# Value, query and gate projections in 512-column matmuls, and all of PSUM opened stage by stage, in a hybrid encoder layer

## The chip, the cores and the metric

The kernel runs on one core of a Trainium2 chip. The metric is device time in microseconds (us) of one execution; a kernel's time is the median of its runs. Engines are named as in the profile: PE is TensorE (PEld its weight load), DVE VectorE, ACT ScalarE, POOL GpSimd, SP SyncE, which issues most DMAs.

## What is computed

One encoder layer over 512 tokens of width 1024, in float32. The part that matters here is the first half:

```python
u = x * (1.0 + sc1) + sh1
proj = u @ w_in[l]
(rq, rff, rfb, ri, rg, aq, ak, av, gate_rec, gate_att) = jnp.split(proj, split_points, axis=-1)
y_rec = hgrn2_bidirectional(rq, rff, rfb, ri, rg, ...) @ w_rec_branch[l]
q = rotary(aq...); k = rotary(ak...); v = av
y_att = windowed_gqa_with_sink(q, k, v, attn_sink[l]) @ w_attn_branch[l]
merged = jax.nn.sigmoid(gate_rec) * y_rec + jax.nn.sigmoid(gate_att) * y_att
```

Then come an output projection with a layer norm, and a convolutional feed-forward block with another. `ri` are the values of the recurrent mixer (512 features), `rg` its output gate (512), `aq` the queries of the attention (512), `ak` and `av` its keys and values (128 each), `rff`, `rfb` and `rq` forget gates and queries of the recurrence (4 heads of 128).

## The kernel before, in words

Every product with weights is done in three matmuls: activations and weights are each split in a rounded part (`hi`, type fp32r, made by ScalarE) and a rest (`lo`, made by VectorE), and `mm3` (L118) adds hi x hi, hi x lo and lo x hi in PSUM. Weights come by DMA as tiles of 1 MB (`w_tile`, two buffers) and are split in two pieces of 128x1024 (`w_split`, L109; four buffers each for hi and lo).

The program has four parts in time. The **head** (to L330) computes the modulation and `u`, and with it the first projections, for heads 0 and 1 of the recurrence, into six PSUM banks `first0` to `first5` (L305). The **scan** (L781 to L796) does the recurrence for two pairs of heads (`scan_pair`, L622): seven levels of 64-column products (`pl`, one pair of banks each, two pairs in turn), then state products (`kt`, `st`) and outputs (`po`). Its VectorE work per level (multiplying `kb` and `qb` by the totals, and masked copies out of PSUM) needs longer than its matmuls. So the remaining projections run between the levels as a **background stream** (`Stream`, L382): a list of items, each with a load and a generator of steps of three matmuls. `scan_pair` yields a number of nanoseconds (STEP is 4600, STEPD 3400, STEPK 4000, STEPS 2600, STEPA 4200; LEAD 13600 stands ahead of the scan), and `drive` (L424) runs as many steps as fill it by the estimate that each step yields. When an item starts, the load of the next is issued. `bg.until(n)` runs the stream until n items are done. Then comes the **attention** (L808 to L993), which uses up the rest of the stream, and then the rest of the layer.

Two kinds of items exist. `proj_fm` (L353) computes features by tokens: weights stationary, 512 tokens moving, one bank of 512 columns over 8 steps. `proj_tm` (L366) computes tokens by features: a token block of `u` stationary, 256 columns of weights moving. A bank holds two token blocks of 256 features, so an item of 256 features is 32 steps, 96 matmuls, two banks. Seven items are of this kind: values (2), keys and values of the attention (1), queries (2), output gate (2). Their results leave PSUM by `use_v`, `use_kv`, `use_q`, `use_rg` (L738 to L756).

PSUM has eight banks of 512 float32 columns. A pool `ps` (L81) with three banks, tag `mm`, lives through the kernel and serves the stream. The five others are opened anew in each stage (`psum_stage`, L84): `ps_start` (two `sc` and three `at` banks), `ps_scan` (two pairs and one `sc`), `ps_rest` (three `at`, two `sc`). A tile scheduler orders the instructions of ScalarE, VectorE and GpSimd by priorities and sets the waits; matmuls marked `kp` stay in program order.

Of the kernel before, what the change touches and what calls it, by code (L numbers as in the profile page):

```python
# [8 lines left out]
F32 = mybir.dt.float32  # L9
F32R = mybir.dt.float32r  # L10
I32 = mybir.dt.int32
AF = mybir.ActivationFunctionType
# [4 lines left out]
P = 128  # L17
# [44 lines left out]
def encoder_layer(  # L62
# [18 lines left out]
    ps = ctx.enter_context(tc.tile_pool(name="ps", bufs=3, space=PSUM))  # L81
# [8 lines left out]
    def mm_ps(name):  # L90
        return ps.tile([P, 512], F32, tag="mm", name=name, bufs=3)
# [11 lines left out]
    banks["sc"] = 2  # L103
# [33 lines left out]
    with tc.tile_pool(name="st", bufs=1) as st:  # L137
# [168 lines left out]
        for p in range(len(pieces)):  # L306
# [3 lines left out]
            if not more:  # L310
                raw = w_tile()
                kp(nc.sync.dma_start(raw.rearrange("p (k n) -> p k n", n=256), w_in_k[:, :, C_RI:C_RI + 256]))
# [3 lines left out]
            else:  # L316
                lows(p, u32)
                ri_parts = w_split_late(raw)
# [47 lines left out]
    def proj_tm(use):  # L366
# [13 lines left out]
        return steps  # L380

# [42 lines left out]
    def drive(fg):  # L424
        for ns in fg:
            bg.run(ns)
# [93 lines left out]
    with tc.tile_pool(name="mx", bufs=1) as mx:  # L520
# [217 lines left out]
        def use_v(hh):  # L738
            return lambda b, a: nc.scalar.copy(v_rec[:, 2 * b:2 * b + 2, 256 * hh:256 * hh + 256], a)
# [5 lines left out]
        def use_q(i):  # L745
            return lambda b, a: nc.scalar.copy(
                qk_raw[:, 2 * b:2 * b + 2, 4 * i:4 * i + 4].rearrange("p b h d -> p b (h d)"), a)

        def use_rg(hh):
            def use(b, a):  # L750
                th = hp.tile([P, S], F32, tag="th", name="th", bufs=2)
                tv = th.rearrange("p (i n) -> p i n", i=2)
                nc.scalar.activation(tv, a, AF.Tanh, scale=0.5)
                nc.vector.scalar_tensor_tensor(out=rgs[:, 2 * b:2 * b + 2, 256 * hh:256 * hh + 256], in0=tv,
                                               scalar=1.0, in1=a, op0=ALU.add, op1=ALU.mult)
            return use  # L756

        ri_load = lambda: ri_parts
        bg.add(ri_load, proj_tm(use_v(0)))
# [3 lines left out]
        bg.add(load_cols(C_RI + 256), proj_tm(use_v(1)))  # L763
        bg.add(load_cols(C_AK), proj_tm(use_kv))
        bg.add(load_cols(C_AQ), proj_tm(use_q(0)))
        bg.add(load_cols(C_AQ + 256), proj_tm(use_q(1)))
        for hh in range(2):
            bg.add(load_cols(C_RG + 256 * hh), proj_tm(use_rg(hh)), ada_hook)
# [13 lines left out]
        banks["sc"] = 1  # L782
        bg.run(LEAD)
        drive(scan_pair(0, 1, lambda L: None))
        cos2, sin2 = rotary_tables()
        bg.until(5)
# [565 lines left out]
```

## Time and profile before

| | us |
|---|---|
| median of 3 runs | 804.8 (803.76 to 805.15) |
| the profiled execution | 803.86 |
| its span, first to last instruction | 802.1 |
| TensorE busy | 782.2 (98%) |
| VectorE busy | 559.6 (70%) |
| ScalarE busy | 358.4 (45%) |
| GpSimd busy | 71.2 (9%) |

A busy TensorE is not one at its peak: a matmul's row lasts from its start to its modelled end, some 390 ns for 512 columns, while the next one starts earlier. The distance between starts is what a matmul costs when they follow each other. In the rows, times are in us from the span's start unless marked ns; `<-` before a name in brackets says what ended the engine's idle time.

### The profile page before, as it was taken

How to read it: one execution, taken by the hardware profiler on the slowest of the kernel's cores; microseconds unless marked ns; L12 is line 12 of the kernel's file. 1: busy time of each engine (PE TensorE's matmuls, PEld its weight loads, DVE VectorE, ACT ScalarE, POOL GpSimd, SP SyncE). 2: the span in 40 equal slices, each digit the busy share in tenths (PEclk: the TensorE clock that was granted, in tenths of full speed). 3: DMA queues.
4: the chain of work that ended last, by engine and by line, in shares of the span. 5: the costliest groups of instructions: out<-in, count | busy, mean ns of one | idle time of the engine just before them, and what ended most of it. 6: DMA issues, size and time to landing. Idle time of an engine off the chain costs nothing.

```text
span 802.1 us, 11578 instructions
## 1 busy us (share of the span) xinstructions
PE 782.2 (98%) x4606; PEld 660.8 (82%) x4606; DVE 559.6 (70%) x881; ACT 358.4 (45%) x576; POOL 71.2 (9%) x98
## 2 busy tenths in 40 slices
PE   5999999999999999999999999999999999999996
PEld 4779889999878777788889988888888888888885
DVE  5879994699486756648766787777665677546437
ACT  3565754653276575533345544434544444112120
POOL 3340000000000000200000683000000000000000
PEclk9999999999999999999999999999999999999999
DMA  9983331122543503686403343464423333332302
GB/s 270 301 231 93 107 105 54 53 83 78 158 145 118 158 1 105 234 222 231 130 29 106 88 123 105 157 210 106 134 80 102 105 105 132 106 105 79 105 1 105
DMA packets 110757, 99.45 MB, mean 124 GB/s; under 512 B 3452, under 2 KB 98032, under 8 KB 110704
## 3 DMA queue, kind: packets, MB, share of 16 engines
q1 hardware_dynamic: 109024, 94.38, 39.7%
q0 software_dynamic: 1664, 4.33, 1.7%
q8 instruction: 36, 0.59, 0.3%
q14 instruction: 17, 0.14, 0.1%
q10 hardware_dynamic: 16, 0.00, 0.0%
HBM read 96.61 MB, written 2.10 MB: 123 GB/s over the span
## 4 chain that ended last, share of the span: by engine, by line
PE 93%; DVE 3%; DMA 1%; ACT 1%; SPq 1%; issue 0%; DVEq 0%
PE up L121 10%; PE up L120 10%; PE up L119 10%; PE dn L119 5%; PE dn L120 5%; PE dn L121 5%; PE fm L119 5%; PE fm L121 5%; PE fm L120 5%; PE tm L119 4%; PE tm L121 3%; PE tm L120 3%; PE pl L618 2%; PE wo L119 2%; PE wo L121 2%; PE wo L120 2%
## 5 line engine op out<-in xcount | busy, mean ns | idle before, releaser
L114 DVE TENSOR_TENSOR w_lo<-raw,w_hi 128x1024 fp32r<-128x1024 f32 x114 | 140.6, 1247 | 103.8 <-ACT w_hi L113 103.7
L113 ACT CAST w_hi<-raw 128x1024 fp32r<-128x1024 f32 x114 | 118.6, 1050 | 146.9 <-PE dn L121 76.0
L119 PE MATMUL up<-u_hi,w_hi 128*128 128x512 f32 (+1 forms) x384 | 142.8, 372 | 0.0
L120 PE MATMUL up<-u_lo,w_hi 128*128 128x512 f32 (+1 forms) x384 | 142.6, 371 | 0.0
L121 PE MATMUL up<-u_hi,w_lo 128*128 128x512 f32 (+1 forms) x384 | 142.6, 371 | 0.0
L120 PEld LDWEIGHTS up<-u_lo,w_hi 128*128 128x128 f32 x384 | 72.3, 188 | 12.6
L119 PEld LDWEIGHTS up<-u_hi,w_hi 128*128 128x128 f32 x384 | 72.3, 188 | 12.5
L121 PEld LDWEIGHTS up<-u_hi,w_lo 128*128 128x128 f32 x384 | 72.3, 188 | 12.4
L119 PE MATMUL dn<-w_hi,g_hi 128*128 128x512 f32 (+1 forms) x198 | 72.5, 366 | 0.0
L120 PE MATMUL dn<-w_lo,g_hi 128*128 128x512 f32 (+1 forms) x198 | 72.5, 366 | 0.0
L121 PE MATMUL dn<-w_hi,g_lo 128*128 128x512 f32 (+1 forms) x198 | 72.4, 366 | 0.0
L119 PE MATMUL fm<-u_hi,w_hi 128*128 128x512 f32 x176 | 70.4, 400 | 0.0
L121 PE MATMUL fm<-u_hi,w_lo 128*128 128x512 f32 x176 | 68.8, 391 | 0.0
L120 PE MATMUL fm<-u_lo,w_hi 128*128 128x512 f32 x176 | 68.8, 391 | 0.0
L119 PE MATMUL tm<-w_hi,u_hi 128*128 128x256 f32 x224 | 64.8, 289 | 0.0
L121 PE MATMUL tm<-w_hi,u_lo 128*128 128x256 f32 x224 | 63.3, 283 | 0.0
L120 PE MATMUL tm<-w_lo,u_hi 128*128 128x256 f32 x224 | 63.3, 283 | 0.0
L437 DVE SCALAR_TENSOR_TENSOR ada<-raw,silu_c,ada 128x1024 f32<-128x1024 f32 x32 | 41.0, 1282 | 12.5 <-DMA raw<-in_w_ada_dram 12.2
L1215 ACT CAST g_hi<-cv 128x512 fp32r<-128x512 f32 x22 | 13.7, 621 | 69.1 <-DVE cv L1214 69.1
L119 PEld LDWEIGHTS tm<-w_hi,u_hi 128*128 128x128 f32 x224 | 42.8, 191 | 0.8
L120 PEld LDWEIGHTS tm<-w_lo,u_hi 128*128 128x128 f32 x224 | 43.0, 192 | 0.1
L121 PEld LDWEIGHTS tm<-w_hi,u_lo 128*128 128x128 f32 x224 | 42.9, 191 | 0.0
(284 smaller groups left out, 1448.9 us busy)
## 6 DMA issues: line engine op xcount, KB each, us to landing
raw<-in_w_up_dram SPq DMA_DIRECT2D x44, 512.0 KB, 5.3
raw<-in_w_ada_dram SPq DMA_DIRECT2D x16, 1024.0 KB, 5.3
raw<-in_w_in_dram SPq DMA_DIRECT2D x15, 1024.0 KB, 5.3
raw<-in_w_down_dram SPq DMA_DIRECT2D x10, 1024.0 KB, 5.0
aw<-in_w_ada_dram SPq DMA_DIRECT2D x32, 256.0 KB, 5.3
raw<-in_w_out_dram SPq DMA_DIRECT2D x4, 1024.0 KB, 4.8
wq<-in_w_in_dram SPq DMA_DIRECT2D x24, 128.0 KB, 4.8
raw<-in_w_in_dram SPq DMA_DIRECT2D x6, 512.0 KB, 4.7
```

The lines of the kernel that those rows point to most:

```text
L113: nc.scalar.copy(hi[:, 0:n], raw[:, o:o + n])
L114: nc.vector.tensor_tensor(out=lo[:, 0:n], in0=raw[:, o:o + n], in1=hi[:, 0:n].bitcast(F32), op=ALU.subtract)
L119: pin(nc.tensor.matmul(o, lhsT=sh, rhs=mh, start=start, stop=False))
L120: pin(nc.tensor.matmul(o, lhsT=sh, rhs=ml, start=False, stop=False))
L121: pin(nc.tensor.matmul(o, lhsT=sl, rhs=mh, start=False, stop=stop))
L437: nc.vector.scalar_tensor_tensor(out=acc, in0=raw[:, j * D:(j + 1) * D], scalar=silu_c[:, 2 * k2 + j:2 * k2 + j + 1], in1=acc, op0=ALU.mul ...
L618: kp(nc.tensor.matmul(dst[64 * a:64 * a + 64, q_:q_ + 64], lhsT=keys[:, k_:k_ + 64], rhs=queries[:, q_:q_ + 64], start=True, stop=True, ti ...
L1215: nc.scalar.copy(g_hi[i], cv[0])
```

## The change

Values, queries and output gate become three pairs of half items. An item of a pair loads four of the eight 128-row blocks of the weights, 512 columns wide (`load_wide`), and adds their products for all four token blocks into four banks (`proj_wide`); the second item of the pair adds the other four row blocks, and each bank leaves PSUM as soon as it is complete. Each step is three matmuls of 512 columns and yields 680. The pool `ps` is gone: the `mm` banks belong to the stage, three in `ps_start`, four in `ps_scan` (whose `sc` bank goes), three in `ps_rest`. The item that the head prepares is now keys and values of the attention, with the two value items behind it; then follow, as before, the features of heads 2 and 3, then queries and gate. The counts in `until` and `need` follow the new list.

```diff
--- before.py
+++ after.py
@@ -78,7 +78,6 @@
     cn = ctx.enter_context(tc.tile_pool(name="cn", bufs=1))
     wp = ctx.enter_context(tc.tile_pool(name="wp", bufs=4))
     big = ctx.enter_context(tc.tile_pool(name="big", bufs=1))
-    ps = ctx.enter_context(tc.tile_pool(name="ps", bufs=3, space=PSUM))
     banks = {}
 
     def psum_stage(name):
@@ -88,7 +87,7 @@
         banks["pool"] = banks["ctx"].enter_context(tc.tile_pool(name=name, bufs=1, space=PSUM))
 
     def mm_ps(name):
-        return ps.tile([P, 512], F32, tag="mm", name=name, bufs=3)
+        return banks["pool"].tile([P, 512], F32, tag="mm", name=name, bufs=banks["mm"])
 
     def sc_ps(name):
         return banks["pool"].tile([P, 512], F32, tag="sc", name=name, bufs=banks["sc"])
@@ -100,7 +99,7 @@
         return banks["pool"].tile([P, 2, 512], F32, tag="pair", name=name, bufs=2)
 
     psum_stage("ps_start")
-    banks["sc"] = 2
+    banks["sc"], banks["mm"] = 2, 3
 
 
     def w_tile():
@@ -309,13 +308,13 @@
             more = p + 1 < len(pieces)
             if not more:
                 raw = w_tile()
-                kp(nc.sync.dma_start(raw.rearrange("p (k n) -> p k n", n=256), w_in_k[:, :, C_RI:C_RI + 256]))
+                kp(nc.sync.dma_start(raw.rearrange("p (k n) -> p k n", n=256), w_in_k[:, :, C_AK:C_AK + 256]))
             if more:
                 nxt = prepare_w(p + 1)
                 acc = gather(p + 1, lambda: lows(p, u32))
             else:
                 lows(p, u32)
-                ri_parts = w_split_late(raw)
+                kv_parts = w_split_late(raw)
             mms = first_mm(p, parts)
             for _ in range(SPLIT[p]):
                 next(mms)
@@ -378,6 +377,34 @@
                             use(b, acc.rearrange("p (i n) -> p i n", i=2))
                         yield 327
         return steps
+
+    def load_wide(col, kh):
+        def load():
+            raw = w_tile()
+            nc.sync.dma_start(raw.rearrange("p (k n) -> p k n", n=512), w_in_k[:, 4 * kh:4 * kh + 4, col:col + 512])
+            return [w_split(raw, 1024 * h, first=False) for h in range(2)]
+        return load
+
+    def proj_wide(use):
+
+        accs = []
+
+        def half(kh):
+            def steps(parts):
+                for tb in range(NTB):
+                    t = slice(tb * P, (tb + 1) * P)
+                    if kh == 0:
+                        accs.append(mm_ps(f"tw{tb}"))
+                    for j in range(4):
+                        k = 4 * kh + j
+                        hi, lo = parts[j // 2]
+                        n = slice((j % 2) * 512, (j % 2) * 512 + 512)
+                        mm3(accs[tb], u_hi[:, k, t], u_lo[:, k, t], hi[:, n], lo[:, n], k == 0, k == KT - 1, kp)
+                        if k == KT - 1:
+                            use(tb, accs[tb])
+                        yield 680
+            return steps
+        return half(0), half(1)
 
     class Stream:
         def __init__(self):
@@ -735,37 +762,33 @@
                                          accum_out=rstat[:, tb, h:h + 1])
                 nc.scalar.copy(o_tok[:, :, h], po[:, e].rearrange("p (b d) -> p b d", d=P))
 
-        def use_v(hh):
-            return lambda b, a: nc.scalar.copy(v_rec[:, 2 * b:2 * b + 2, 256 * hh:256 * hh + 256], a)
+        def use_v(tb, a):
+            nc.scalar.copy(v_rec[:, tb], a)
 
         def use_kv(b, a):
             nc.scalar.copy(qk_raw[:, 2 * b:2 * b + 2, 8:10].rearrange("p b h d -> p b (h d)"), a[:, :, 0:128])
             nc.scalar.copy(v_att[:, 2 * b:2 * b + 2], a[:, :, 128:256])
 
-        def use_q(i):
-            return lambda b, a: nc.scalar.copy(
-                qk_raw[:, 2 * b:2 * b + 2, 4 * i:4 * i + 4].rearrange("p b h d -> p b (h d)"), a)
-
-        def use_rg(hh):
-            def use(b, a):
-                th = hp.tile([P, S], F32, tag="th", name="th", bufs=2)
-                tv = th.rearrange("p (i n) -> p i n", i=2)
-                nc.scalar.activation(tv, a, AF.Tanh, scale=0.5)
-                nc.vector.scalar_tensor_tensor(out=rgs[:, 2 * b:2 * b + 2, 256 * hh:256 * hh + 256], in0=tv,
-                                               scalar=1.0, in1=a, op0=ALU.add, op1=ALU.mult)
-            return use
-
-        ri_load = lambda: ri_parts
-        bg.add(ri_load, proj_tm(use_v(0)))
+        def use_q(tb, a):
+            nc.scalar.copy(qk_raw[:, tb, 0:8].rearrange("p h d -> p (h d)"), a)
+
+        def use_rg(tb, a):
+            th = hp.tile([P, S], F32, tag="th", name="th", bufs=2)
+            nc.scalar.activation(th, a, AF.Tanh, scale=0.5)
+            nc.vector.scalar_tensor_tensor(out=rgs[:, tb], in0=th, scalar=1.0, in1=a, op0=ALU.add, op1=ALU.mult)
+
+        first_load = lambda: kv_parts
+        wide_v, wide_q, wide_g = proj_wide(use_v), proj_wide(use_q), proj_wide(use_rg)
+        bg.add(first_load, proj_tm(use_kv))
+        for kh in range(2):
+            bg.add(load_wide(C_RI, kh), wide_v[kh])
         for h in (2, 3):
             bg.add(load_cols(C_RFF + h * P, C_RFB + h * P), proj_fm(lambda f, a, h=h: gate_f(f, h, a)))
             bg.add(load_half(C_RQ + h * P), proj_fm(lambda f, a, h=h: silu_q(h, a), nf=1))
-        bg.add(load_cols(C_RI + 256), proj_tm(use_v(1)))
-        bg.add(load_cols(C_AK), proj_tm(use_kv))
-        bg.add(load_cols(C_AQ), proj_tm(use_q(0)))
-        bg.add(load_cols(C_AQ + 256), proj_tm(use_q(1)))
-        for hh in range(2):
-            bg.add(load_cols(C_RG + 256 * hh), proj_tm(use_rg(hh)), ada_hook)
+        for kh in range(2):
+            bg.add(load_wide(C_AQ, kh), wide_q[kh])
+        for kh in range(2):
+            bg.add(load_wide(C_RG, kh), wide_g[kh], ada_hook)
         gr_a = yin.tile([P, 2, S], F32, name="gr_a")
         gr = [gr_a[:, i] for i in range(2)]
 
@@ -779,25 +802,25 @@
             gate_f(1, j, first[2 + j])
             silu_q(j, first[4 + j])
         psum_stage("ps_scan")
-        banks["sc"] = 1
+        banks["mm"] = 4
         bg.run(LEAD)
-        drive(scan_pair(0, 1, lambda L: None))
+        drive(scan_pair(0, 3, lambda L: None))
         cos2, sin2 = rotary_tables()
-        bg.until(5)
+        bg.until(7)
 
         def turn_qk(L):
             if L == 64:
                 bg.until(9)
                 rope(range(2))
 
-        drive(scan_pair(1, 6, turn_qk))
+        drive(scan_pair(1, 3, turn_qk))
         rope(range(2, 4))
         bg.until(11)
         dump("qk_raw", qk_raw)
 
         hp_ctx.close()
         psum_stage("ps_rest")
-        banks["sc"] = 2
+        banks["sc"], banks["mm"] = 2, 3
 
         grp_pool = ph1.enter_context(tc.tile_pool(name="grp", bufs=1, side="right"))
         gr_b = grp_pool.tile([P, KT - 2, S], F32, name="gr_b")
```

**The opening of the scan's stage, TensorE.** `first0` to `first5` are the head's accumulators, `tm0` is the first bank of the stream's first item. Before:

```order
L294 MATMUL first4_233<-u_lo_71,w_hi_555 128x512
L294 MATMUL first5_234<-u_lo_71,w_hi_555 128x512
L119 MATMUL tm0_741<-w_hi_610,u_hi_70 128x256 [waits Activation_49]
L120 MATMUL tm0_741<-w_lo_611,u_hi_70 128x256 [waits DVE_49]
L121 MATMUL tm0_741<-w_hi_610,u_lo_71 128x256
```

and now:

```order
L293 MATMUL first4_230<-u_lo_68,w_hi_552 128x512
L293 MATMUL first5_231<-u_lo_68,w_hi_552 128x512
L118 MATMUL tm0_737<-w_hi_607,u_hi_67 128x256 [waits DVE_49,PE_49]
L119 MATMUL tm0_737<-w_lo_608,u_hi_67 128x256
L120 MATMUL tm0_737<-w_hi_607,u_lo_68 128x256
```

`tm0` has moved from the pool that lives through the kernel to the first place in the new stage's pool; its first matmul waits for VectorE's count 124 and for TensorE's `first5`, where it waited for ScalarE's tanh of `first0`. VectorE's order there is the same as before but for line numbers; row 124 of the list, the reader of `first5`, is the sixth of these:

```order
L616 SCALAR_TENSOR_TENSOR lvl_mask_675<-xf_681,xg_682 128x128 [waits DVE_49]
L626 TENSOR_SCALAR f0_701<-th_713,f_mul_643,f_add_644 128x512 [waits Activation_49]
L626 TENSOR_SCALAR f0_701<-th_716,f_mul_643,f_add_644 128x512 [waits Activation_49]
L571 TENSOR_SCALAR ang_1524<-inv_1491,pos_f_1489 128x32 [waits Pool_49]
L659 TENSOR_SCALAR kb0_866<-f0_701 128x2048 [waits DVE_49]
L636 SCALAR_TENSOR_TENSOR q0_708<-th_719,first5_231 128x512 [waits Activation_49]
L660 TENSOR_TENSOR ks0_868<-kb0_866 128x1024 [waits DVE_49]
L637 TENSOR_SCALAR q0_708<-q0_708 128x512 [waits DVE_49]
```

These are gates and queries of heads 0 and 1 (`th` is a tanh of ScalarE) and the first operations of `scan_pair`.

**ScalarE behind it.** `qk_raw` and `v_att` take `tm0` out of PSUM; `kc` and `qc` are copies of level 1 and 2 of the scan. Before (where the first item was values, `v_rec`):

```order
L598 ACTIVATE th_719<-first3_232 128x512 [waits DVE_49]
L739 COPY v_rec_658<-tm0_741 128x2x256 [waits PE_49]
L608 ACTIVATE th_722<-first5_234 128x512 [waits DVE_49]
L670 COPY kc0_1_914<-kb0_863 128x1024 [waits DVE_49]
L113 CAST w_hi_843<-raw_841 128x1024 [waits DMAHW4_49,PE_49]
L739 COPY v_rec_658<-tm1_791 128x2x256 [waits PE_49]
L113 CAST w_hi_939<-raw_936 128x1024 [waits DMAHW6_49,DMAHW5_49]
```

and now:

```order
L625 ACTIVATE th_716<-first3_229 128x512 [waits DVE_49]
L635 ACTIVATE th_719<-first5_231 128x512 [waits DVE_49]
L697 COPY kc0_1_910<-kb0_866 128x1024 [waits DVE_49]
L697 COPY qc0_1_911<-qb0_867 128x1024 [waits DVE_49]
L697 COPY qc0_2_971<-qb0_867 128x1024 [waits DVE_49]
L769 COPY qk_raw_660<-tm0_737 128x2x128 [waits PE_49,Activation_49]
L770 COPY v_att_661<-tm0_737 128x256
```

The copies out of `tm0` stood ahead of the tanh of `first5` and of `kc`, and now stand behind both `qc`.

**The opening of the attention's stage, TensorE.** `fm` are features of a gate, `pk0` the transposes of the first keys. Before:

```order
L119 MATMUL fm0_2503<-u_hi_70,w_hi_2317 128x512
L120 MATMUL fm0_2503<-u_lo_71,w_hi_2317 128x512
L121 MATMUL fm0_2503<-u_hi_70,w_lo_2318 128x512
L833 MATMUL pk0_2525<-ident_72,kk0_2519 128x128 [waits PE_49,Activation_49]
L833 MATMUL pk0_2525<-ident_72,kk0_2519 128x128
```

and now:

```order
L118 MATMUL fm1_2107<-u_hi_67,w_hi_1895 128x512
L119 MATMUL fm1_2107<-u_lo_68,w_hi_1895 128x512
L120 MATMUL fm1_2107<-u_hi_67,w_lo_1896 128x512
L856 MATMUL pk0_2201<-ident_69,kk0_2194 128x128 [waits Activation_49]
L856 MATMUL pk0_2201<-ident_69,kk0_2194 128x128
```

The `fm` that runs ahead of `pk0` is now one that began in the scan's stage (`fm1`), and `pk0` waits for its reader on ScalarE.

## Rows read from the trace of the kernel before

**Rows 1.** The page: the chain that ended last, shares of the span by engine.

```profile
PE 93%; DVE 3%; DMA 1%; ACT 1%; SPq 1%; issue 0%; DVEq 0%
```

**Rows 2.** TensorE's timeline where the head ends: start us, us, engine, line, op, out<-in, shapes, count.

```profile
57.15 1.52 PE L294 MATMUL first<-u_lo,w_hi 128*128 128x512 f32 x6
58.51 0.28 PE L119 MATMUL tm<-w_hi,u_hi 128*128 128x256 f32 x1
```

**Rows 3.** TensorE in the scan: timeline of `tm` and `fm`; the page's group of narrow matmuls.

```profile
69.90 0.28 PE L121 MATMUL tm<-w_hi,u_lo 128*128 128x256 f32 x1
...
99.97 0.40 PE L120 MATMUL fm<-u_lo,w_hi 128*128 128x512 f32 x1
...
104.06 0.39 PE L120 MATMUL fm<-u_lo,w_hi 128*128 128x512 f32 x1
...
L119 PE MATMUL tm<-w_hi,u_hi 128*128 128x256 f32 x224 | 64.8, 289 | 0.0
```

**Rows 4.** TensorE's timeline in the output projection: two `wo` matmuls, four apart.

```profile
400.76 0.39 PE L120 MATMUL wo<-w_lo,m_hi 128*128 128x512 f32 x1
...
401.67 0.39 PE L121 MATMUL wo<-wo_hi,m_lo 128*128 128x512 f32 x1
```

**Rows 5.** VectorE's timeline after the head.

```profile
58.42 1.21 DVE L114 TENSOR_TENSOR w_lo<-raw,w_hi 128x1024 fp32r<-128x1024 f32 x1
...
66.42 1.22 DVE L632 TENSOR_SCALAR kb<-f 128x2048 f32<-128x2048 f32 x1
67.56 0.68 DVE L609 SCALAR_TENSOR_TENSOR q<-th,first 128x512 f32<-128x512 f32 x1
68.16 1.22 DVE L633 TENSOR_TENSOR ks<-kb 128x1024 f32<-128x1024 f32 x1
```

**Rows 6.** ScalarE's timeline: a `v_rec` copy, the last tanh of `first`, `qc` of level 2.

```profile
65.31 0.58 ACT L739 COPY v_rec<-tm 128x512 f32<-128x512 f32 x1
65.94 0.60 ACT L608 ACTIVATE th<-first 128x512 f32<-128x512 f32 x1
...
77.69 1.16 ACT L670 COPY qc<-qb 128x1024 f32<-128x1024 f32 x1 [1.33 <-DVE qb L660]
```

**Rows 7.** TensorE at the head, then windows at the end: us, busy by engine, PEclk, DMA.

```profile
11.00 0.80 PE L296 MATMUL first<-u_hi,w_hi 128*128 128x512 f32 x1 [1.17 <-ACT u_hi L262]
...
16.13 0.79 PE L296 MATMUL first<-u_hi,w_hi 128*128 128x512 f32 x1
...
18.00 0.63 PE L296 MATMUL first<-u_hi,w_hi 128*128 128x512 f32 x1
18.43 0.63 PE L297 MATMUL first<-u_hi,w_lo 128*128 128x512 f32 x1
18.85 2.15 PE L294 MATMUL first<-u_lo,w_hi 128*128 128x512 f32 x6
20.85 0.39 PE L296 MATMUL first<-u_hi,w_hi 128*128 128x512 f32 x1
...
794.00:798.00 4.00, 0.86 (x8) 0.65 (x6) 3.54 (x11) 0.20 (x1) 0.00 (x0) 1.00 0.34 128
798.00:802.00 4.00, 0.00 (x0) 0.00 (x0) 1.30 (x4) 0.00 (x0) 0.00 (x0) 0.55 0.37 131
```

**Rows 8.** TensorE's timeline at the attention's first transposes: [idle before <-releaser] at the end.

```profile
223.97 0.39 PE L121 MATMUL fm<-u_hi,w_lo 128*128 128x512 f32 x1
224.55 0.44 PE L833 MATMUL pk<-ident,kk 128*128 128x128 f32 x2 [0.19 <-ACT kk L819]
225.84 0.33 PE L833 MATMUL pk<-ident,kk 128*128 128x128 f32 x1 [0.85 <-DVE kk L820]
```

**Rows 9.** TensorE's timeline in the scan: two levels' products.

```profile
84.36 1.15 PE L618 MATMUL pl<-qc,kc 128*64 128x64 f32 x32
...
91.11 1.09 PE L618 MATMUL pl<-qc,kc 128*64 128x64 f32 x30
```

**Rows 10.** VectorE's timeline in the scan: the masked copy of a level.

```profile
86.60 1.50 DVE L678 COPY_PREDICATED sc<-lvl_mask,pl 64x512 f32<-64x512 int32 x2
```

## The prediction

> **What bounds the kernel now.** First the page's busy shares and its chain of waits: the chain that ended last runs over TensorE for 93% of the span [rows 1]. So a gain or a loss counts where TensorE issues matmuls or stands still, and other engines count where TensorE waits for them. Next the list of TensorE's matmuls with their starts, over the stretch that the change rewrites. The head ends with six matmuls of `first`, and the first `tm` follows at 58.51 us without a gap [rows 2]. From there to `pk` at 224.55 us the starts follow each other at the pace of the matmuls; the first waits to see are those at `pk` [rows 8]. So in this stretch the end moves one for one with TensorE's issue time. Then the paces. A 512-column `fm` starts every (104.06 - 99.97)/18 = 0.227 us; a 256-column `tm` every (69.90 - 58.51)/95 = 0.120 us, which is 0.240 us for 512 columns [rows 2, 3]. A narrow matmul therefore costs some 6 ns that the wide form pays once where the narrow one pays twice. That is all that width alone can give. Last, VectorE and ScalarE around 58 to 69 us, because the order of the changed program makes TensorE wait for them there.
>
> **The change, part by part.**
>
> *Wide projections.* The 672 `tm` matmuls [rows 3] are seven items of 96; the change keeps one (keys and values of the attention) and turns six, 576 matmuls, into three pairs of half items with 3 x 96 = 288 of 512 columns. Today 576 x 0.120 = 69.1 us. The new ones have the same orientation as `wo` (activations stationary, weights moving, 512 columns), and `wo` starts every (401.67 - 400.76)/4 = 0.2275 us [rows 4], so 288 x 0.227 = 65.4 us. Term: -3.7 us, between -3.3 and -4.1 for 1 to 2 ns in either pace. The section "Wait — 56ns, not 53.3ns?" of the Trainium skill's page "TensorE: Matmul & The Clock Gate" has it otherwise: columns over 2.4 GHz plus about 2.5 ns, from which I estimate 109.2 and 215.8 ns and a gain of 0.7 us. The rows show about twice that fixed part in this fp32r kernel, and the measurement decides.
>
> *PSUM by stage.* Before, the first tile of the scan's own pool was `pd0`, and `tm` took banks of a pool that lives through the kernel. Now all eight banks belong to the stage, and the first tile of the new pool is the first item's `tm0`. In the order above, its first matmul carries a wait for VectorE and for TensorE itself. VectorE's count there, 124, is reached by `q0<-th,first5`: the last reader of the old pool, although `tm0` lies in bank 0, which `first5` never used. So TensorE stands still until VectorE has done that instruction. VectorE's order up to it is the same before and after, and no instruction in it depends on `tm`. In the trace VectorE works without a pause from 58.42 us through two weight splits, masks, gates and `kb`, and starts that `q` at 67.56 us; it takes 0.68 us [rows 5]. ScalarE's input for it, the second tanh of `first` for q, starts at 65.94 us behind a `v_rec` copy that moves away [rows 6], but VectorE's `kb` at 66.42 us stands ahead of `q` anyway, so the end at 68.24 us stays. TensorE starts `tm` at about 68.3 instead of 58.5 us. Term: +9.8 us, between +9.3 (VectorE half a microsecond earlier without the copy) and +10.2. Nothing covers it: queued behind that wait is the whole stream of matmuls, and everybody in the scan waits for those.
>
> *TensorE's clock after standing still.* At the head 512-column matmuls start 0.43 us apart at 18.00 and 18.43 us [rows 7], in the scan 0.227 us [rows 3]: the 1.2 and the 2.4 GHz level. (The granted clock in the windows reads 1.00 there, so the spacing is what tells.) At the low level the engine had been idle or broken; it had then run without a break since 16.13 us, and the rise fell near 20.2 us (six matmuls from 18.85 to 20.85 us are 3 slow and 3 fast ones by their sum). At the end of the program the granted clock reads 0.55 from 798 us, after TensorE's last 0.86 us of work in the four microseconds before [rows 7]. Here it would have stood for 9.8 us, so I take it that `tm` starts at 1.2 GHz. If the rise again takes 4.1 us, matmuls at 0.213 us (half of 0.427) instead of 0.120 lose 44% of it: +1.8 us. Bounds: 0 (the clock stays up), and 44% of the 9.2 us from the head's first `first` matmul at 11.00 us to the rise, 4.0 us. I take 1.8, from the one unbroken run that is shown.
>
> *The order of items and the shorter levels.* From one `pl` to the next the scan takes 91.11 - 84.36 = 6.75 us today [rows 9]. With steps of 680 ns seven steps fill STEP, so a level under wide steps is 21 x 0.227 and one `pl` of 1.15 us, 5.9 us. VectorE's share of a level is two `copy_predicated`, 1.5 us [rows 10], `kb` and `qb` at 1.2 each, as other operations of their size [rows 5], and one weight split of 1.2 us: 5.1 us, with some 1.3 us of rope in the second pair. That is close to a level, but `pl`'s inputs are made two levels ahead, and the standstill gives VectorE a lead of nearly two more. Cost 0, at worst 0.5 us for each of seven levels of the second pair, rounded to +2 us for those that outlast the lead. The gates of heads 2 and 3 now come late in the first pair: the last feeds `pd1` through tanh, two small VectorE operations, some 2 us, behind 21 stream matmuls and `po`, 9 us. Covered; were it not, at most +1.
>
> *The second opening, at the attention.* `pk0` now waits for the tanh of the last `fm` of that item, read from the old pool. Today `pk` already starts 0.58 us after the last `fm`, 0.35 more than a pace, and its third transpose some 1.05 us late, for ScalarE and VectorE [rows 8]. By the new order ScalarE does the sums of squares, kk, qq, one split and that tanh; with the durations of today it ends 0.9 us after TensorE arrives. So one wait of 0.9 takes the place of 1.4: 0, between -1.4 and +1.0. DMAs, splits and PSUM reads keep their number and size (1 MB loads, 512-column copies); after the attention the rows of TensorE are the same, and cost nothing.
>
> **Sum.** The profiled execution took 803.9 us (span 802.1). 803.9 - 3.7 + 9.8 + 1.8 = 811.8 us. The median of the runs shown, 804.8, lies 0.9 above that execution, so for a median I give **812.7 us**, 1.0% slower.
>
> **The rivals.**
>
> *The opening holds nothing up (the other side).* If the wait on `tm0` were over at 58.5 us (the count belonging to an earlier instruction than I read), TensorE would run into the next one: `tw2` takes the bank of `tm0`, and ScalarE's copies of `tm0` now stand behind `qc` of level 2, whose copy starts at 77.69 us and takes 1.16 us [rows 6]; without the two splits that sat ahead of it on VectorE it could end about 77.3. The two copies add 0.7, and `tw2` would be ready at 58.5 + 11.5 + 24 x 0.227 = 75.5. It would lose 2.6 us: 804.8 - 3.7 + 2.6 = 803.7, no change that can be told. It decides if the wait at `tm0` is under 1 us. For it: bank 0 was long free. Against it: the order's row with its wait on VectorE. Chance 0.06.
>
> *Neither wait bites.* Then only the width is left: 801.1 us, faster. ScalarE's order speaks against it. Chance 0.05.
>
> *Width gives nothing.* If the 6 ns belong to this orientation's columns and not to each matmul, 288 x 0.240 = 69.1 us, and the time is 816.4 us. `wo` at 0.2275 [rows 4] speaks against it. Chance 0.03. The skill's formula, above, would end nearby, at an estimated 815.7 us.
>
> **How the numbers follow.** The forecast has 0.86. Its low end: 804.8 - 4.1 + 9.3 + 0 - 1.4 = 808.6; its high end: 804.8 - 3.3 + 10.2 + 4.0 + 2.0 = 817.7, where all bounds meet. The range 808.0 to 817.0 holds nearly all of it and the third rival, and leaves out the first two. 0.2% is 1.6 us, about what a measurement of this kernel can tell from no change. Slower: 0.86 + 0.03 = 0.89. Within 0.2%: the first rival, 0.06. Faster: the second, 0.05.
>
> **What would show it.** In the profile after, a gap of nearly 10 us before the first `tm` put down to VectorE's q operation; `tm` starts 0.21 us apart for some microseconds, then 0.12; `tw` starts 0.227 us apart; no other gap over 1 us up to `pk`; and levels of 5.9 us under `tw`. The prediction is wrong if `tm` follows `first` within a microsecond, if the narrow and wide paces are equal per column, or if gaps appear at `pl` or `tw` that add up to more than 2 us.

## The result and the profile after

Median of three runs 812.45 us (811.61 to 813.88) against 804.8 (803.76 to 805.15): a ratio of 1.0094, 95% interval 1.0074 to 1.0114. Six more runs beside the experiments gave 812.6 us and 1.0093 (1.0072 to 1.0115). The prediction was 812.7 us, slower, with a range of 808 to 817. The profiled execution took 812.45 us, span 810.7, which is 8.6 more than before.

The page after: TensorE's busy row, the granted clock over 40 slices, and the chain, which answers to [rows 1].

```profile
PE 780.2 (96%) x4318; PEld 646.3 (80%) x4318; DVE 560.9 (69%) x881; ACT 356.5 (44%) x574; POOL 71.3 (9%) x98
...
PEclk9997999999999999999999999999999999999999
...
PE 92%; DVE 3%; DMA 2%; ACT 1%; SPq 1%; issue 0%; POOL 0%; POOLq 0%; DVEq 0%
```

One slice of the clock row stands out, the fourth, 61 to 81 us. The waits of TensorE (for what, us in total, times, longest us) say what lies there:

```profile
PE tm L118 <- DVE q L636: 10.4, 1, 10.4
...
PE pk L856 <- ACT gr_a L796: 0.7, 1, 0.7
```

The first was forecast, down to the instruction that ends it; it has no counterpart before, when `tm` followed the head at once [rows 2]. TensorE's timeline there:

```profile
57.76 1.52 PE L293 MATMUL first<-u_lo,w_hi 128*128 128x512 f32 x6
...
69.68 0.55 PE L118 MATMUL tm<-w_hi,u_hi 128*128 128x256 f32 x1 [10.40 <-DVE q L636]
70.03 0.42 PE L119 MATMUL tm<-w_lo,u_hi 128*128 128x256 f32 x1
70.25 0.41 PE L120 MATMUL tm<-w_hi,u_lo 128*128 128x256 f32 x1
...
74.51 0.38 PE L119 MATMUL tm<-w_lo,u_hi 128*128 128x256 f32 x1
74.73 0.28 PE L120 MATMUL tm<-w_hi,u_lo 128*128 128x256 f32 x1
74.84 0.28 PE L118 MATMUL tm<-w_hi,u_hi 128*128 128x256 f32 x1
74.96 0.28 PE L119 MATMUL tm<-w_lo,u_hi 128*128 128x256 f32 x1
```

The last `first` matmul starts at 58.89 and `tm` 10.79 us later; before that distance was 0.23. Then `tm` starts lie 0.213 us apart up to 74.7 us, and 0.12 from there. The windows of the same stretch (busy by engine, granted clock, DMA share, GB/s) show it as the 1.2 GHz level (0.50), which had begun inside the standstill:

```profile
59.50:64.40 4.90, 0.00 (x0) 0.00 (x0) 4.27 (x13) 0.86 (x1) 2.34 (x32) 1.00 0.68 224
64.50:69.60 5.10, 0.00 (x0) 0.00 (x0) 5.10 (x14) 3.01 (x5) 0.00 (x0) 0.50 0.71 195
69.70:74.70 5.00, 5.00 (x23) 5.00 (x24) 5.00 (x6) 1.04 (x2) 0.00 (x0) 0.50 0.00 0
74.80:83.40 8.60, 8.60 (x74) 8.60 (x74) 7.86 (x29) 4.07 (x6) 0.00 (x0) 1.00 0.01 2
```

VectorE over the standstill (compare [rows 5]) has the same instructions in the same order, with one pause that was not there before:

```profile
59.02 1.21 DVE L113 TENSOR_TENSOR w_lo<-raw,w_hi 128x1024 fp32r<-128x1024 f32 x1
...
63.84 0.17 DVE L565 CAST pos_f<-pos_i 128x4 f32<-128x4 int32 x1 [0.60 <-DMA pos_i<-in_positions_dram]
...
67.72 1.22 DVE L659 TENSOR_SCALAR kb<-f 128x2048 f32<-128x2048 f32 x1
68.85 0.68 DVE L636 SCALAR_TENSOR_TENSOR q<-th,first 128x512 f32<-128x512 f32 x1
```

`q` ends at 69.53 and `tm` starts 0.15 us later. Further on, from TensorE's timeline: the wide pace (compare [rows 3, 4]), two levels of the scan [rows 9], and the transposes of the attention [rows 8].

```profile
96.46 1.15 PE L645 MATMUL pl<-qc,kc 128*64 128x64 f32 x32
...
99.26 0.39 PE L119 MATMUL tw<-w_lo,u_hi 128*128 128x512 f32 x1
...
102.21 0.39 PE L120 MATMUL tw<-w_hi,u_lo 128*128 128x512 f32 x1
102.53 1.15 PE L645 MATMUL pl<-qc,kc 128*64 128x64 f32 x32
...
230.03 0.39 PE L120 MATMUL fm<-u_hi,w_lo 128*128 128x512 f32 x1
...
231.15 0.66 PE L856 MATMUL pk<-ident,kk 128*128 128x128 f32 x4 [0.72 <-ACT gr_a L796]
```

The two `tw` shown stand thirteen starts apart: (102.21 - 99.26)/13 = 0.227 us. A level now takes 6.07 us where it took 6.75. Added up over TensorE's list of starts, so that each product carries the pause behind it, the two spans differ like this (us):

| stretch | before | after | difference |
|---|---|---|---|
| to the last `first` | 58.28 | 58.89 | +0.61 |
| from there to the first `tm` | 0.23 | 10.79 | +10.56 |
| `tm` and `tw`: 672 / 96 + 288 | 82.88 | 13.79 + 68.20 | -0.89 |
| `ao` and `pt` | 17.35 | 16.38 | -0.97 |
| `pk` and `fm` | 126.07 | 125.45 | -0.62 |
| `yr` and the rest up to the first `ya` | 76.76 | 76.31 | -0.45 |
| from `ya` to the end | 440.52 | 440.86 | +0.34 |

The 96 `tm` at the head of the stream take 11.51 us where the clock is up (the pool-for-life run below) and 13.79 here: the lower clock costs 2.28 us. Without that, `tm` and `tw` are 79.72 us, 3.16 less than before.

### The profile page after: what moved, and what is told of

Same layout as the page of the kernel before. It is cut to its first block, busy times and chain, and to the rows that moved or that the text cites. A ratio compares the mean times of both kernels' runs of the same rounds, so it can differ in the third digit from the quotient of the medians.

```text
span 810.7 us, 11003 instructions
## 1 busy us (share of the span) xinstructions
PE 780.2 (96%) x4318; PEld 646.3 (80%) x4318; DVE 560.9 (69%) x881; ACT 356.5 (44%) x574; POOL 71.3 (9%) x98
## 4 chain that ended last, share of the span: by engine, by line
PE 92%; DVE 3%; DMA 2%; ACT 1%; SPq 1%; issue 0%; POOL 0%; POOLq 0%; DVEq 0%
PE up L119 10%; PE up L118 10%; PE up L120 10%; PE dn L118 5%; PE dn L119 5%; PE dn L120 5%; PE fm L118 5%; PE fm L120 5%; PE fm L119 5%; PE tw L118 3%; PE tw L120 3%; PE tw L119 3%; PE pl L645 2%; PE wo L118 2%; PE wo L120 2%; PE wo L119 2%
## 5 line engine op out<-in xcount | busy, mean ns | idle before, releaser
L118 PEld LDWEIGHTS dn<-w_hi,g_hi 128*128 128x128 f32 x198 | 37.3, 189 | 6.7 <-issue 0.6
L120 PEld LDWEIGHTS dn<-w_hi,g_lo 128*128 128x128 f32 x198 | 37.3, 188 | 6.2
L119 PEld LDWEIGHTS dn<-w_lo,g_hi 128*128 128x128 f32 x198 | 37.4, 189 | 6.0
L118 PE MATMUL tw<-w_hi,u_hi 128*128 128x512 f32 x96 | 38.8, 405 | 0.0
L120 PEld LDWEIGHTS fm<-u_hi,w_lo 128*128 128x128 f32 x176 | 33.1, 188 | 7.1
L118 PEld LDWEIGHTS fm<-u_hi,w_hi 128*128 128x128 f32 x176 | 33.1, 188 | 6.1
```

What stands on the lines that cost most here:

```text
L118: pin(nc.tensor.matmul(o, lhsT=sh, rhs=mh, start=start, stop=False))
L119: pin(nc.tensor.matmul(o, lhsT=sh, rhs=ml, start=False, stop=False))
L120: pin(nc.tensor.matmul(o, lhsT=sl, rhs=mh, start=False, stop=stop))
```

## The experiments

Ten runs followed, of seven new kernels and, once more, of three old ones. Each ratio is against runs of the kernel before on the same chip (medians 806.2, 805.5 and 804.7 us in the three sets). The time up to the last `first` varies from one execution to the next (56.97 to 60.95 us in the profiles, 1.3 us of it between two profiles of the unchanged kernel), so the table also gives the stretch from there to TensorE's last product, which is 736.30 us before.

| kernel | median us | ratio, 95% interval | last `first` to end, against before |
|---|---|---|---|
| before again, one execution | 803.7 | | +1.1 |
| after (again) | 812.6 | 1.0093 (1.0072 to 1.0115) | +7.9 (+7.4) |
| pool for life | 798.4 | 0.9902 (0.9884 to 0.9919) | -5.5 |
| the same again | 799.0 | 0.9925 (0.9906 to 0.9944) | -5.5 |
| stages alone | 820.1 | 1.0164 (1.0141 to 1.0187) | +14.8 |
| first readers early | 810.7 | 1.006 (1.004 to 1.008) | +5.6 |
| warm | 810.6 | 1.0058 (1.0038 to 1.0077) | +6.1 |
| order alone | 804.3 | 0.9982 (0.9966 to 0.9998) | -1.4 |
| opening later | 800.6 | 0.995 (0.9932 to 0.9968) | -3.6 |
| warm head | 798.6 | 0.992 (0.9901 to 0.9939) | -5.6 |

The first row shows what the last column can tell. In that execution of the unchanged kernel the head ended early, at 56.97 us, and the first `tm` came 1.13 us after it, with 0.7 us of waiting for a tanh of ScalarE. So about 1 us in this column says little by itself. From the first `tm` to the first `ya` the two profiles of the unchanged kernel agree within 0.12 us (303.07 and 303.19).

**The change with a pool for life.** Three accumulator banks are again outside the stages; the wide pair's fourth comes from the scan's score bank.

```diff
+    ps = ctx.enter_context(tc.tile_pool(name="ps", bufs=3, space=PSUM))
...
-        return banks["pool"].tile([P, 512], F32, tag="mm", name=name, bufs=banks["mm"])
+        return ps.tile([P, 512], F32, tag="mm", name=name, bufs=3)
...
-                        accs.append(mm_ps(f"tw{tb}"))
+                        accs.append(mm_ps(f"tw{tb}") if tb < 3 else sc_ps(f"tw{tb}"))
...
-        banks["mm"] = 4
+        banks["sc"] = 1
...
```

> The change with its 512-wide projections and its new order of items, but the pool of three accumulator banks lives through the whole kernel again, as before the change; the fourth accumulator of a wide pair, tw3, is taken from the one score bank that the scan's stage then has. By my theory (the new pool's first tile waits for the last reader of the old pool) the first tm waits for nothing long: the wait tm <- VectorE q of 10.4 us goes, with it the 2.27 us that the lower clock costs the products behind it, and the gain of the wide products (3.2 to 3.8 us) stays: 804.8 - 3.5 = 801.3 us, between 800.0 and 803.0, faster than the kernel before. The rival (the wait comes from the wide pairs or from the order of the items): still 811 to 813 us. A second rival: the waits of tw2 for ScalarE's copies of tm0 behind qc take the place of the standstill: about 805 us, with a gap of some us before tw2.

TensorE's timeline at the end of the head:

```profile
58.07 1.07 PE L294 MATMUL first<-u_lo,w_hi 128*128 128x512 f32 x4
58.98 0.28 PE L119 MATMUL tm<-w_hi,u_hi 128*128 128x256 f32 x1
```

The standstill and the slow products are gone, and no wait at `tw` takes their place: 0.9902, faster than expected (798.4 us, below the 800.0 of the range). From the first `tm` to the first `ya` the stretch is 5.8 us shorter than before; the wide products were to give 3.5 of it. The rest is the subject of the run on the order.

**The stages alone.** The kernel before, narrow and in its old order, with the three banks moved into the stages. This run asks whether opening the banks by stage makes the standstill by itself.

```diff
-    ps = ctx.enter_context(tc.tile_pool(name="ps", bufs=3, space=PSUM))
...
-        return ps.tile([P, 512], F32, tag="mm", name=name, bufs=3)
+        return banks["pool"].tile([P, 512], F32, tag="mm", name=name, bufs=3)
```

> The kernel before with its 256-wide projections and its order of items, but with PSUM opened by stage altogether: the three accumulator banks are a part of each stage's pool. By my theory the first tm waits for VectorE's q as in the change, some 10 us in place of nothing, and the products behind it run for about 10 us at a lower clock, for 2.2 us more; nothing is won by width: 804.8 + 10.0 + 2.2 = 817.0 us, between 814.5 and 818.5. The rival (the opening alone costs nothing; the wide pairs or the order do it): 804 to 805.5 us.

The waits of TensorE, then its timeline at the attention:

```profile
PE tm L118 <- DVE q L608: 9.7, 1, 9.7
...
PE fm L118 <- ACT gr_a L772: 3.0, 1, 3.0
```

```profile
236.22 0.50 PE L118 MATMUL fm<-u_hi,w_hi 128*128 128x512 f32 x1 [3.05 <-ACT gr_a L772]
236.56 0.39 PE L119 MATMUL fm<-u_lo,w_hi 128*128 128x512 f32 x1
236.79 0.41 PE L120 MATMUL fm<-u_hi,w_lo 128*128 128x512 f32 x1
237.02 0.61 PE L118 MATMUL fm<-u_hi,w_hi 128*128 128x512 f32 x1
237.42 0.63 PE L119 MATMUL fm<-u_lo,w_hi 128*128 128x512 f32 x1
237.85 0.63 PE L120 MATMUL fm<-u_hi,w_lo 128*128 128x512 f32 x1
```

Opening alone costs the standstill: `tm` starts 9.9 us later after the head than before. The ratio lies within what was expected (1.0164 x 804.8 = 818.0 us; the median itself, 820.1, is above the range), but the profile is 14.8 us longer where I had reckoned 12.2. The lower clock costs the `tm` only 1.5 us here (84.40 us for all 672, before 82.88); what makes up for it is that the second opening bites too. The first `fm` of the attention's stage waits for the tanh `gr_a`, the last reader of the scan's banks. ScalarE did that one only at 235.49 us, behind eight sums of squares with their reads and two copies of 0.6 us for the scan's output. Then the clock falls, and the next `fm` start 0.43 us apart. In the change the same kind of wait cost 0.7 us: there the last `fm` of the old stage (at 230.03) comes 4.7 us after the last `po`, when ScalarE is through with that work (at 228.83) and has `kk`, `qq` and a weight split left; here it comes 0.6 us after it (232.79 for 232.21). What an opening costs is thus a question of what else stands in the last reader's queue.

**First readers early.** The six readers of the head's accumulators get a higher priority in the scheduler.

```diff
-        for j in range(2):
-            gate_f(0, j, first[j])
...
+        with tc.high_priority():
+            for j in range(2):
+                gate_f(0, j, first[j])
...
```

> The change, with the six readers of the first head's accumulators (gates and silu) given a higher priority, which puts VectorE's last reader q ahead of four instructions that stood before it: two on masks, one on angles, and kb (1.14 us), and nothing else. By my theory the first tm comes as much earlier as q does, 1.2 to 2 us, and the time falls by the same, to 810.4 to 811.3 us. The rival (the first tm waits for something else that ends at about the same time, a transfer or the pool itself): the gap stays at 10.4 us and the time at 812.4 us, within 0.1 %.

VectorE's timeline, and the first `tm` of TensorE's:

```profile
67.31 0.68 DVE L636 SCALAR_TENSOR_TENSOR q<-th,first 128x512 f32<-128x512 f32 x1
...
68.58 1.22 DVE L659 TENSOR_SCALAR kb<-f 128x2048 f32<-128x2048 f32 x1
```

```profile
68.14 0.55 PE L118 MATMUL tm<-w_hi,u_hi 128*128 128x256 f32 x1 [8.72 <-DVE q L636]
```

Counted from the end of the head, `q` comes 1.7 us earlier and so does `tm`; it still starts 0.15 us after `q` has ended. The median, 810.7 us, lies in the range that was expected, but the kernel before was 1.4 us slower in this set than the 804.8 behind that range; by the ratio (1.006 x 804.8 = 809.6 us) it ends 0.8 us below that range, and by the profile it fell by 2.3 us against the change and 1.8 against its repetition. 1.7 us of that are the wait. So `tm` hangs on that instruction, and not on something that ends near it.

**Warm.** Forty products that nobody uses, into a spare bank, ahead of the scan's opening.

```diff
+        warm = sc_ps("warm")
+        for i in range(40):
+            kp(nc.tensor.matmul(warm, lhsT=u_hi[:, 0, 0:P], rhs=u_hi[:, i % KT], start=True, stop=True))
         psum_stage("ps_scan")
```

> The change, with 40 products of 512 columns of data already there, into a spare bank of the first stage, put on TensorE before the scan's stage opens: 40 x 0.227 = 9.1 us of work that nobody uses, inside the standstill of 10.4 us. By my theory the standstill stays (the first tm still begins when VectorE's q has ended), but TensorE is not idle in it, the granted clock stays at 1.00 and the first 23 tm no longer take 0.21 us each: 812.45 - 2.27 = 810.2 us, between 809.7 and 810.7. The rival (the slow tm come from something else, such as the accumulators' readers): 812.4 us and 0.21 us each as before. If the added products push the first tm later, the time is longer by what they stick out.

```profile
66.63 1.52 PE L806 MATMUL warm<-u_hi 128*128 128x512 f32 x6
69.39 0.35 PE L118 MATMUL tm<-w_hi,u_hi 128*128 128x256 f32 x1 [1.24 <-DVE q L636]
69.58 0.28 PE L119 MATMUL tm<-w_lo,u_hi 128*128 128x256 f32 x1
69.70 0.28 PE L120 MATMUL tm<-w_hi,u_lo 128*128 128x256 f32 x1
...
69.70:74.70 5.00, 5.00 (x44) 5.00 (x43) 5.00 (x6) 1.06 (x2) 0.00 (x0) 1.00 0.01 3
```

`tm` still waits for `q`, but starts 0.12 us apart at once, and the granted clock reads 1.00 in all four windows of the stretch (the last row is the one that had 0.50 in the change). From the first `tm` to the first `pd` it takes 18.50 us in place of 20.71. That is the clock's share, 2.2 us, separated from the wait's. The median of 810.6 us lies in the range that was expected, and the ratio's 1.0058 x 804.8 = 809.4 us just below it.

**The order alone.** The kernel before, narrow and with its pool for life, with the change's order of items.

```diff
...
+        bg.add(first_load, proj_tm(use_kv))
+        bg.add(load_cols(C_RI), proj_tm(use_v(0)))
+        bg.add(load_cols(C_RI + 256), proj_tm(use_v(1)))
         for h in (2, 3):
...
-        bg.add(load_cols(C_RI + 256), proj_tm(use_v(1)))
-        bg.add(load_cols(C_AK), proj_tm(use_kv))
...
-        drive(scan_pair(0, 1, lambda L: None))
+        drive(scan_pair(0, 3, lambda L: None))
...
```

> The kernel before (256-wide products, one pool of three accumulators for life) with only the change's order of items: keys and values of the attention first, then V, the gates of the heads 2 and 3, the queries, the output gate. In the run with the pool for life the stretch from the first tm to the first ya was 5.8 us shorter than before the change, of which 3.16 us are the wide products; 2.6 us are left, most of them about pk, ao and yr in the attention. If they come from the order of the items (the attention's own waits fall at other places), this kernel gains them: 804.8 - 2.5 = about 802 us, a ratio of 0.996 to 0.998, and pk no longer waits 1 us. The prediction's own term (the order costs nothing or up to 2 us): a ratio of 1.000 to 1.0025. If they come from the wide products after all (fewer steps in the attention to wait for): 1.000, and pk waits 1 us as before.

VectorE's and TensorE's timelines:

```profile
64.96 0.17 DVE L538 CAST pos_f<-pos_i 128x4 f32<-128x4 int32 x1 [0.75 <-DMA pos_i<-in_positions_dram]
...
226.52 0.60 PE L833 MATMUL pk<-ident,kk 128*128 128x128 f32 x4
```

A ratio of 0.9982, just outside what was expected (0.996 to 0.998), with an interval that ends close to 1; by the profile the gain is 1.4 us, and 1.5 from the first `tm` to the first `ya`. `pk` no longer waits (16 `pk` take 1.58 us for 2.71 before), and `yr` gives 0.3. `ao` and `pt` stay at 17.34 us; they fall to 16.4 in the wide kernels only. So the 5.8 us of the pool-for-life run are some 1.5 us of order, 3.16 of width in the products themselves, and 0.95 in `ao` and `pt`. The last is no price of a wide product: no pair runs there (in the change the last `tw` starts at 211.96 us, the first `pt` at 256.55). What differs is where the stream's `fm` fall: in the narrow kernels one stands between the last eight `ao`, in the wide ones none. That this is the whole of it, and that the coarser steps cause it, was not tried.

VectorE's row shows something else: the pause for the positions, which the change has too, is already here, in a narrow kernel with a pool for life. It comes with the order of items, and not with the width or the opening.

**The opening later.** The first item, keys and values, still goes into the first stage's banks; the scan's stage opens behind it.

```diff
+        bg.until(1)
         psum_stage("ps_scan")
         banks["mm"] = 4
-        bg.run(LEAD)
+        bg.run(LEAD - 32 * 327)
```

> The change, with the scan's PSUM stage opened one item later: the 96 tm (the first item, 96 x 0.120 = 11.5 us) still go into the first stage's three accumulators, and stand behind the head at once; the lead of the scan is shorter by as many steps, so that TensorE's order stays the same. By my theory the opening is then covered: while VectorE works through its list to q (some 10 us), TensorE has those 96 tm. What the first tile of the new stage (tw0) now waits for is the last reader of the old one, ScalarE's copy of the second tm tile, 0.5 to 1.5 us after the last tm. So the standstill of 10.4 us becomes one of about 1 us at tw0, no product runs at the lower clock, and the time is 812.45 - 10.4 - 2.3 + 1.0 = 800.8 us, between 799 and 802.5. The rival (opening a stage costs a standstill of 10 us wherever it stands): 810 us and more, with the gap at tw0.

TensorE's timeline at the new opening, and ScalarE's ahead of it:

```profile
72.57 0.28 PE L120 MATMUL tm<-w_hi,u_lo 128*128 128x256 f32 x1
74.16 0.50 PE L118 MATMUL tw<-w_hi,u_hi 128*128 128x512 f32 x1 [1.32 <-ACT v_att L770]
```

```profile
71.05 1.57 ACT L697 COPY kc<-kb 128x1024 f32<-128x1024 f32 x1 [1.14 <-DVE kb L659]
72.49 1.06 ACT L112 CAST w_hi<-raw 128x1024 fp32r<-128x1024 f32 x1
73.44 0.39 ACT L769 COPY qk_raw<-tm 128x256 f32<-128x256 f32 x1
73.70 0.41 ACT L770 COPY v_att<-tm 128x256 f32<-128x256 f32 x1
```

The median, 800.6 us, lies where it was expected. The 10.4 us become 1.3, with the change's own allocation of banks: the opening costs what of the old stage's readers is not covered by work that TensorE can already do. By the profile this is 1.9 us behind the pool for life, which has neither this wait nor the 0.7 us at `pk` (0.2 us there, for VectorE's `kk`).

**Why the first median ran ahead of its profile.** The pool-for-life kernel was 7.9 us faster by the medians, 5.5 by the profiles. Of the kernel before, the eleven runs of the last set fall in two groups: three of 807.1 to 808.1 us with a mean granted clock of 0.994, and eight of 803.3 to 804.9 with 0.997 or 0.998. Some profiles show a fall of the clock in the head, for instance that of the opening later (timeline, and a window with the granted clock at 0.50):

```profile
42.13 0.40 PE L227 MATMUL pm<-ones,acc 128*64 128x1 f32 x8 [3.19 <-DVE acc L219]
...
42.98 0.63 PE L296 MATMUL first<-u_hi,w_lo 128*128 128x512 f32 x1
43.40 0.63 PE L295 MATMUL first<-u_hi,w_hi 128*128 128x512 f32 x1
...
43.00:44.00 1.00, 1.00 (x4) 0.80 (x3) 1.00 (x3) 0.99 (x2) 0.00 (x0) 0.50 1.12 310
```

The unchanged kernel, run once more on the experiments' chip, was to say where its longer time lies:

> The kernel before once more, unchanged, for a profile from the chip on which the experiments ran. Its time there had a median of 806.2 us in place of 804.8. If the 1.4 us more lie in one stretch (the waits for transfers in the head), the run with the pool for life, measured at a ratio of 0.9902 but only 5.0 us shorter by the profiles, is to be read against that; if it is spread or does not show, the two stay apart by about 2 us that the profiles do not explain.

That execution took 803.7 us and is one without the fall, so it could not show it; what it shows is how far the head's length moves on its own, and that against this profile the pool for life is 6.6 us shorter and not 5.5. Repeating both changed kernels was the better test of whether the surplus is only that.

> The kernel with the pool for life once more, unchanged. From the last products of first to the end its profile is 5.5 us shorter than the profile before the change, but by the medians it was 7.9 us faster. In three of the profiles so far (the PSUM stage alone, the order alone, the opening one item later) the granted clock falls to 0.50 for some 4 us in the head, after a wait of 3.2 us for VectorE's acc before pm; in the others that wait is 2.3 us and the clock stays. If the surplus of 2.4 us is only how often that fell into the runs of either kernel, the ratio now comes out nearer to 1 - 5.5/804.8 = 0.9932, between 0.991 and 0.995. If the surplus belongs to this kernel, 0.990 again.

> The change once more, unchanged, beside the others on one chip. From the last products of first to the end its profile is 7.9 us longer than the one before the change, so a ratio of 1.0099; measured in three runs: 1.0094. Expected: 1.008 to 1.011.

0.9925 and 1.0093: as expected. (The waits named in the first of the two were 2.30, 2.76 and 3.19 us in the three profiles with the fall, and up to 2.73 in those without it, so 3.2 against 2.3 is no dividing line.) This time two of six runs of the pool for life had a clock of 0.995. Its gain is about 6 us.

**Warm head.** The pool for life, with eight unused products in that wait of the head.

```diff
...
                 pm = sc_ps(f"pm{p}")
+                if p == WARM_AT:
+                    for _ in range(8):
+                        kp(nc.tensor.matmul(pm, lhsT=u_hi[:, 0, 0:P], rhs=u_hi[:, 0], start=True, stop=True))
...
```

> The kernel with the pool for life, and in the head, ahead of the sixth pm, eight products of 512 columns that nobody uses (8 x 0.227 = 1.8 us) written into pm's own bank before it is begun: they lie in the wait for VectorE's acc of 2.3 to 3.2 us. If a standstill of some 3 us there is what makes the clock fall in some executions, none of this kernel's executions has it: its slowest run comes down to near its fastest (a spread under 2.5 us, mean granted clock 0.997 or more in each) and the median is as that of the kernel without them in its quick runs, 797 to 799 us. If the falls have another cause, runs with a clock of 0.994 to 0.996 remain. If the products stick out, the time is up to 1 us longer.

```profile
38.28 2.08 PE L242 MATMUL pm<-u_hi 128*128 128x512 f32 x8
41.23 0.40 PE L229 MATMUL pm<-ones,acc 128*64 128x1 f32 x8 [0.87 <-DVE acc L221]
```

The products fit into the wait, and five of six runs lie at 798.0 to 798.8 us. But one has 800.3 us at a clock of 0.995, and the ratio, 0.992, is that without them. Whether they remove one cause of two or were merely lucky five times is open. I do not count it as a gain.

## Why the prediction was right

- **PSUM by stage, +9.8 us:** 10.56, above its upper bound of 10.2. Mechanism, place and the instruction that ends it were as forecast, and three runs show it: opening alone brings the standstill, moving `q` moves `tm`, and covering it with the first item takes it away. The mis-sized part is the 0.60 us that VectorE waited for the positions, and 0.15 us from the end of `q` to `tm`. I had copied VectorE's list without a pause from before; the 2 KB transfer landed after 4.0 us there and after 5.3 in the change. The order alone has this pause too (0.75 us), so it comes with the order of items, whose term does not have it.
- **The clock, +1.8 us:** 2.28, and 2.2 by the warm run. `tm` ran at 1.2 GHz for 5.0 us after the standstill, where I had taken 4.1 from the head. That this came near is in part luck: the four profiles with the standstill have 5.0, 4.7 (the repetition), 4.0 (first readers early) and 3.3 us (stages alone), so one stretch from the head does not fix it.
- **Wide, -3.7 us:** 3.16 in `tm` and `tw`, below my lower bound of 3.3. A wide product starts every 0.227 us, as `wo` did, but with the switches to and from the scan's products the 288 `tw` come to 68.20 us where I had 65.4, and the narrow ones they replace to 71.4 where I had 69.1. The 0.97 in `ao` and `pt` come on top and stand in no term of mine. The formula of the Trainium skill's page "TensorE: Matmul & The Clock Gate", section "Wait — 56ns, not 53.3ns?", would have left an estimated gain of 0.7 us; the rows disagree with it. They do so by more than I wrote: 2 x 0.1199 - 0.2272 = 0.0126 us is what a product pays whatever its width, five times that formula's part and not twice; the "6 ns" halve it by mistake. The term went by the two paces and does not change.
- **Order of items, 0, at worst +2:** this was a gain of some 1.4 us, by the profile of the run on the order. I had bounded only a loss, and put the end of `pk`'s old wait under the second opening. The levels came out at 6.07 us for 5.9 and held nobody up.
- **Second opening, 0 (-1.4 to +1.0):** a wait of 0.7 at `pk`; `pk` and `fm` together take 0.6 us more than with the pool for life. The wait was forecast (0.9), but most of what I had it replace falls to the order. With the old order the same opening costs 3 us and then the clock.
- **The sum:** forecast +7.9 for the median; measured +7.65, and +7.9 in the profile from the end of the head on. Wait and clock came out 1.2 us above their terms and width gave 0.5 less; against that, `ao` and `pt` gave 1.0, and order and second opening together 1.1 where I had 0. So the sum is as near as it is because errors of some 2 us cancelled. Its high end left out the second opening's +1.0, with which it is 818.7.
- **The rivals:** whether `tw2` would wait for ScalarE's copies behind `qc` can be read only where the opening holds nothing up. With the pool for life there is no wait at `tw`: the copies stand ahead of `qc` there, an order that I had read only for the change. In that kernel the width does what the third rival denied.

## What to carry to other kernels

When a pool that lives through the kernel is folded into stages, look for the first tile of the new stage and the last reader of the old one: in these kernels no matmul of the new stage started before that reader's engine had worked through its own list up to it, though the prediction's reading of the program puts the new tile in a bank that this reader never touched (no trace shows banks). Either keep the tiles that bridge the boundary in a pool of their own (13 us less than the change by the profiles, 5.5 less than the kernel before), or open the stage behind work that the old one can still hold (11.5 and 3.6 us); and price the products after a standstill like these, of 9 to 10 us, at the lower clock (1.5 to 2.3 us here). A gain per instruction, such as wider products, is best measured with the allocation held as it was.

## What the hardware showed

- The granted clock fell 0.8 us after TensorE had resumed from a standstill of 3.05 us (stages alone: `fm` at 236.56 to 237.02 still 0.23 us apart, then 0.43). After standstills of 1.24 and 1.32 us in the runs above it did not fall.
- In the head a wait of 3.19 us was followed by the fall (opening later). One of 2.30 us was followed by it in the run with stages alone and was not in the kernel before; one of 2.76 us was in the order alone, and one of 2.73 in the change was not. So the length of that one wait does not decide it. What does was not found.
- The 2 KB of positions landed 5.2 to 5.4 us after their issue in every kernel with the new order of items, the narrow one of the order alone (5.4) among them, and 3.9 to 4.0 us after it in the three profiles with the old order. Beside them the new order loads 1 MB in one piece where 512 KB pieces ran before; that this is the cause was not tried.
